# First adaLN piece summed on two engines, and w_in loaded in halves: one hybrid decoder layer on one core

## The chip, the core and the metric

One core of a Trainium2 chip runs the whole layer in one launch. TensorE (PE) multiplies, VectorE (DVE) and ScalarE (ACT) do elementwise work, SyncE (SP) issues most DMAs. The metric is the time of one execution in microseconds (us): before, the median of 3 runs is 1309.07 (1307.7 to 1309.66).

## The reference

Sequence 256, model width 2048, float32. `c` has one row, so `mod` is one vector for all positions.

```python
mod = jnp.einsum('bd,de->be', jax.nn.silu(c), w_ada[layer]) + b_ada[layer]
shift, scale, gate = jnp.split(mod, 3, axis=-1)
h = rms_norm(x, g_pre[layer]) * (1.0 + scale[:, None, :]) + shift[:, None, :]
proj = jnp.einsum('bsd,de->bse', h, w_in[layer])
q_mla, kv_a, z_mla, qkv_dil, z_dil, gl_mla, gl_dil = jnp.split(proj, IN_SPLITS, axis=-1)
a = mla_branch(q_mla, kv_a, positions, g_kv[layer], w_kv_b[layer]) * jax.nn.silu(z_mla)
y_mla = jnp.einsum('bse,ed->bsd', a, w_mla_proj[layer])
bb = dilated_branch(qkv_dil, positions) * jax.nn.silu(z_dil)
y_dil = jnp.einsum('bse,ed->bsd', bb, w_dil_proj[layer])
merged = jax.nn.sigmoid(gl_mla) * y_mla + jax.nn.sigmoid(gl_dil) * y_dil
out = jnp.einsum('bsd,de->bse', merged, w_o[layer])
x = x + gate[:, None, :] * rms_norm(out, g_post[layer])
```

w_in has 20032 columns. `mla_branch` is latent attention with 16 heads, `dilated_branch` attention of 8 heads in three groups that are merged by their softmax sums.

## The kernel before, in words

**Chunks.** The 2048 input channels lie in 16 chunks of 128 partitions. `xT[q]` is x transposed, four chunks each. For chunk k, `make_h` (L188 to 200) forms h = xT * colmul * rstdT on DVE, its high part `hTh` with the shift added on ACT (L198), and the low part `hTl` on DVE (L199). Every product of w_in runs three times: high weights by hTh, high by hTl, low by hTh (`multiply`, L237 to 245). A weight tile is loaded by SP (L215), cast to its high part `whi` on ACT (L223) and subtracted to its low part `wlo` on DVE (L224). A load holds up to four chunks of 512 columns (1 MB, `RAW`), in four buffers, and is split in two halves, with four buffers each for whi and wlo.

**Shift and scale.** h needs the columns `colsh` and `colmul` of its chunk, that is, w_ada's columns of this chunk summed over all 16 input chunks with the weights silu(c), `ccol`. `ada_steps(pi)` does this for a piece of several chunks: 16 loads of two blocks (shift, scale), each multiplied by its `ccol` and added on DVE (L164, L166) into `ada`; `finish` then sums over the partitions on PE, one product of one column with `ones` per block (L175), and DVE forms colsh and colmul. `PIECES` gives the chunks of each piece: (2, 2, 2, 2, 4, 4).

**The head.** 16 groups of columns (nine `d`, zd0, two of kva with 256 and 320 columns, zd1, three more `d`; the others 512 wide) are multiplied by the chunks known so far. In stage pi, the `VISITS[pi]` groups that have the fewest chunks are visited; a visit multiplies the chunks that the group lacks, into an accumulator in PSUM (`acc_tile`, two, of two banks each), and the result is copied by ACT at the first visit (L527) and added by DVE at later ones (L529). Between the visits the next piece's steps are issued. The last stage visits all 16 groups; behind zd0 it issues the rotary embedding `rope` (L387 to 390) of six `d` and the first dilated attention, whose products are mixed with the visits that are left.

**Start.** x is loaded in four tiles (L109), transposed by PE (L269) and copied by ACT (L270); DVE sums the squares (L273) and forms rstd by small operations (L128 to 137); `rdiag` (L282) times ones on PE (L285) spreads it to rows, copied to `rstdT`; a transposed table of rows gives biases and gains (`pt_cols`, L290).

**What sets the order.** The engines' instruction lists are static: a scheduler of the framework places the instructions on each engine, as shown below. Engines wait for each other by semaphores, a load also for the release of its buffer by the buffer's last reader.

Of the kernel before, what the change touches and what calls it, by code (L numbers as in the profile page):

```python
# [33 lines left out]
UL = 4  # L34
UK = 2
RAW = UL * 512
HALF = UK * 512
RAW_BUFS = 4
# [5 lines left out]
PIECES = (2, 2, 2, 2, 4, 4)  # L44
VISITS = (11, 9, 7, 16, 16)
# [29 lines left out]
def hybrid_block(ctx: ExitStack, tc: tile.TileContext, x, c, positions, w_ada, b_ada, g_pre, g_post,  # L75
# [8 lines left out]
    ps = ctx.enter_context(tc.tile_pool(name="ps", bufs=1, space=bass.MemoryType.PSUM))  # L84
# [16 lines left out]
    nc.scalar.dma_start(crow, c[0].rearrange("(r p) -> r p", p=P))  # L101
    nc.scalar.dma_start(tid, table[:, 0:T_ZER])
# [42 lines left out]
    def ada_steps(pi):  # L145
# [3 lines left out]
        kb = RAW // (2 * n)  # L149
# [21 lines left out]
        def finish():  # L171
            pt = tp_tile([P, 2, nk], f"pt_ada{pi}")
            for j in range(2):
                for b in range(nk):
                    T.matmul(pt[:, j, b:b + 1], acc[:, j, b * P:(b + 1) * P], ones[:, 0:1],  # L175
                             start=True, stop=True)
            V.tensor_add(colsh[:, a:a + nk], pt[:, 0, :], bsh[:, a:a + nk])
            sc = sp.tile([P, 4], F32, tag="adasc", name=f"adasc{pi}")
            V.tensor_add(sc[:, :nk], pt[:, 1, :], bsc[:, a:a + nk])
# [33 lines left out]
    def load(w, k0, nk, c0, n, name):  # L213
# [48 lines left out]
    for q in range(4):  # L262
# [36 lines left out]
    def gate_sum(n, k0):  # L299

        if k0 == 0 and n % 2 == 0:
# [6 lines left out]
            v, w_ada[0, k0 * P:(k0 + UL) * P, col:col + 512].rearrange("(k p) n -> p k n", p=P))  # L308
        for k in range(UL):
# [20 lines left out]
    gate_todo = [(n, k0) for n in range(4) for k0 in range(0, KC, UL)]  # L330
# [185 lines left out]
    def visit(gi, upto):  # L516
# [19 lines left out]
    for pi in range(len(PIECES)):  # L536
# [4 lines left out]
        if not last:  # L541
            todo = sorted(todo, key=lambda g: (have[g], g))[:VISITS[pi]]
# [65 lines left out]
    for f in range(4):  # L608
# [118 lines left out]
    step = RAW // n  # L727
    tiles = []
    for k0 in range(0, KC, step):
        tiles += load_split(w_o[0], k0, step, c0, n, f"last_{k0}")  # L730
# [36 lines left out]
```

## Time and profile before

| | |
|---|---|
| median of 3 runs | 1309.07 us (1307.7 to 1309.66) |
| profiled execution | 1308.65 us, span 1306.9 us |
| PE busy | 1263.7 us, 97% of the span |
| DVE, ACT busy | 836.7 us (64%), 590.1 us (45%) |
| DMA | 274.97 MB, mean 210 GB/s |

The span reaches from the first to the last recorded instruction. The time given for one PE instruction overlaps the next one, so a pace is read from start to start, or from a piece of the chain of waits; and a busy PE may run at half its clock, which the granted clock tells. Idle time is put down to what ended it.

### The profile page before, as it was taken

To read this page: it belongs to the slowest core of one execution; us is meant where nothing else is said; L and a number is where in the kernel's file an instruction comes from. 1 tells how busy PE (TensorE), PEld (TensorE's weight loads), DVE (VectorE), ACT (ScalarE), POOL (GpSimd) and SP (SyncE) were. 2 spreads that over 40 slices of the span, in tenths; PEclk is the share of its full clock that TensorE was granted. 3 is DMA by queue.
4 is the path that set the end of the run, shared out by engine and by line. 5 is a ranking of instruction groups with operands and counts; after the bars stand their busy time and mean duration, and the time that the engine had idled before them with its cause. 6 is when DMAs were issued, how large, how long until landed. Compare 5 with 4: busy or idle time off the path is not lost.

```text
span 1306.9 us, 16173 instructions
## 1 busy us (share of the span) xinstructions
PE 1263.7 (97%) x6239; PEld 1070.0 (82%) x6239; DVE 836.7 (64%) x1196; ACT 590.1 (45%) x746; POOL 0.2 (0%) x4
## 2 busy tenths in 40 slices
PE   3899999999999999999999999999999999999996
PEld 3688887888888888888889898898888888888886
DVE  7779999988765445539656576655444444565545
ACT  2553433433464444455545555455444444433442
POOL 0000000000000000000000000000000000000000
PEclk7999999999999999999999999999999999999999
DMA  8899988985532555425756486564555555665751
GB/s 282 275 320 300 311 305 283 317 314 170 188 130 97 193 193 194 161 73 192 238 190 238 145 264 232 172 225 160 193 193 194 193 193 193 209 211 192 258 161 65
DMA packets 155224, 274.97 MB, mean 210 GB/s; under 512 B 5830, under 2 KB 46988, under 8 KB 155148
## 3 DMA queue, kind: packets, MB, share of 16 engines
q1 hardware_dynamic: 152732, 268.62, 61.1%
q10 hardware_dynamic: 2416, 5.33, 1.2%
q8 instruction: 49, 0.80, 0.3%
q14 instruction: 27, 0.22, 0.0%
HBM read 271.83 MB, written 2.10 MB: 210 GB/s over the span
## 4 chain that ended last, share of the span: by engine, by line
PE 85%; DVE 6%; DMA 4%; ACT 2%; issue 2%; SPq 0%; DVEq 0%; ACTq 0%
PE acc_d L244 24%; PE acc_mq L244 9%; PE acc_gd L244 7%; PE acc_ym L244 7%; PE acc_gm L244 7%; PE acc_zm L244 7%; PE acc_o L244 6%; PE acc_yd L244 3%; PE acc_kv L244 3%; PE acc_zd L244 3%; DMA raw_d<-in_w_in 2%; DVE ada L166 2%; PE s_D L472 1%; PE pv_D L481 1%; PE acc_kva L244 1%
## 5 line engine op out<-in xcount | busy, mean ns | idle before, releaser
L223 ACT CAST whi_d<-raw_d 128x1024 fp32r<-128x1024 f32 x144 | 149.6, 1052 | 202.3 <-PE acc_d L244 107.0
L224 DVE TENSOR_TENSOR wlo_d<-raw_d,whi_d 128x1024 fp32r<-128x1024 f32 x144 | 174.7, 1222 | 75.1 <-ACT whi_d L223 73.9
L244 PE MATMUL acc_d<-whi_d,hTh 128*128 128x512 f32 x576 | 156.6, 394 | 7.9 <-ACT hTh L198 3.1
L244 PE MATMUL acc_d<-whi_d,hTl 128*128 128x512 f32 x576 | 157.3, 393 | 0.0
L244 PE MATMUL acc_d<-wlo_d,hTh 128*128 128x512 f32 x576 | 155.4, 392 | 0.9 <-DVE wlo_d L224 0.9
L244 PEld LDWEIGHTS acc_d<-whi_d,hTh 128*128 128x128 f32 x576 | 107.9, 189 | 32.0 <-ACT hTh L198 4.1
L244 PEld LDWEIGHTS acc_d<-wlo_d,hTh 128*128 128x128 f32 x576 | 108.5, 189 | 24.0 <-DVE wlo_d L224 1.4
L244 PEld LDWEIGHTS acc_d<-whi_d,hTl 128*128 128x128 f32 x576 | 108.4, 189 | 22.4
L166 DVE SCALAR_TENSOR_TENSOR ada<-raw_a,ccol,ada 128x512 f32<-128x512 f32 (+1 forms) x90 | 83.4, 926 | 5.8 <-DMA raw_a<-in_w_ada 4.5
L224 DVE TENSOR_TENSOR wlo_mq<-raw_mq,whi_mq 128x768 fp32r<-128x768 f32 x64 | 60.9, 956 | 36.7 <-ACT whi_mq L223 22.0
L223 ACT CAST whi_mq<-raw_mq 128x768 fp32r<-128x768 f32 x64 | 53.0, 835 | 55.9 <-PE acc_mq L244 20.0
L224 DVE TENSOR_TENSOR wlo_gm<-raw_gm,whi_gm 128x1024 fp32r<-128x1024 f32 x32 | 39.2, 1225 | 45.4 <-ACT whi_gm L223 45.4
L224 DVE TENSOR_TENSOR wlo_ym<-raw_ym,whi_ym 128x1024 fp32r<-128x1024 f32 x32 | 39.2, 1224 | 34.1 <-ACT whi_ym L223 34.1
L224 DVE TENSOR_TENSOR wlo_gd<-raw_gd,whi_gd 128x1024 fp32r<-128x1024 f32 x32 | 39.2, 1225 | 33.0 <-ACT whi_gd L223 31.3
L244 PE MATMUL acc_mq<-whi_mq,hTl 128*128 128x384 f32 x256 | 59.4, 342 | 0.0
L529 DVE TENSOR_TENSOR d<-d,acc_d 128x1024 f32<-128x1024 f32 x45 | 54.7, 1216 | 7.1 <-PE acc_d L244 7.0
L244 PE MATMUL acc_mq<-wlo_mq,hTh 128*128 128x384 f32 x256 | 57.4, 339 | 0.0
L244 PE MATMUL acc_mq<-whi_mq,hTh 128*128 128x384 f32 x256 | 56.6, 339 | 0.6 <-ACT whi_mq L223 0.6
L224 DVE TENSOR_TENSOR wlo_o<-raw_o,whi_o 128x1024 fp32r<-128x1024 f32 x28 | 34.3, 1225 | 35.3 <-ACT whi_o L223 35.3
L223 ACT CAST whi_ym<-raw_ym 128x1024 fp32r<-128x1024 f32 x32 | 33.8, 1055 | 51.1 <-PE acc_ym L244 44.3
L223 ACT CAST whi_gm<-raw_gm 128x1024 fp32r<-128x1024 f32 x32 | 33.8, 1055 | 49.6 <-PE acc_gm L244 43.9
L223 ACT CAST whi_gd<-raw_gd 128x1024 fp32r<-128x1024 f32 x32 | 33.7, 1053 | 40.7 <-PE acc_gd L244 20.3
(264 smaller groups left out, 2338.9 us busy)
## 6 DMA issues: line engine op xcount, KB each, us to landing
raw_d<-in_w_in SPq DMA_DIRECT2D x63, 1024.0 KB, 4.9
raw_mq<-in_w_in SPq DMA_DIRECT2D x32, 768.0 KB, 4.4
raw_a<-in_w_ada SPq DMA_DIRECT2D x64, 256.0 KB, 5.2
raw_a<-in_w_ada SPq DMA_DIRECT2D x32, 512.0 KB, 6.3
raw_zm<-in_w_in SPq DMA_DIRECT2D x16, 1024.0 KB, 5.0
raw_g<-in_w_ada SPq DMA_DIRECT2D x16, 1024.0 KB, 5.2
raw_gd<-in_w_in SPq DMA_DIRECT2D x16, 1024.0 KB, 4.9
raw_gm<-in_w_in SPq DMA_DIRECT2D x16, 1024.0 KB, 4.8
```

The costliest lines, as they stand in the source:

```text
L166: V.scalar_tensor_tensor(flat, w, ccol[:, kk:kk + 1], flat, op0=ALU.mult, op1=ALU.add)
L223: A.copy(whi[:, :m], raw)
L224: V.tensor_tensor(wlo[:, :m], raw, whi[:, :m].bitcast(F32), ALU.subtract)
L244: T.matmul(acc[:, t, :n], opd.get(part, k0 + k, t), wt[:, k * n:(k + 1) * n], start=start and ph == 0 and k == 0, stop=stop and ph == 2 an ...
L472: T.matmul(sc[:, i * nk:(i + 1) * nk], qk[g][:, 0, t * P:(t + 1) * P], qk[g][:, 1, 0:nk], start=True, stop=True)
L481: T.matmul(pv, pT[:, b, :], dil[2, g, quad][:, kt, hs], start=b == 0, stop=b == nb - 1)
L529: V.tensor_add(d, d, acc[:, :, lo:hi])
```

## The change

- Pieces (3, 2, 3, 2, 2, 2, 2), with visits (8, 8, 7, 7, 7, 9) ahead of the last stage: seven stages in place of six. In the last stage seven groups lack four chunks and nine lack two; before, all sixteen lacked four.
- The first piece has three chunks, and its loads are 128 x 2 x 384, one to a buffer. Even input chunks are accumulated on DVE as before. For odd ones PE multiplies the raw block (stationary) by `ccol` (one column) straight into columns of `pt_ada`, six products each. With the six for DVE's sum there are nine sets of columns, which one reduction on DVE adds.
- Loads hold two chunks of 512 columns at most (512 KB), in eight buffers, in place of four chunks (1 MB) in four. Each load is one split. The loads of `gate_sum` are halved likewise.
- The squares of the first half of x's rows go from DVE to ACT. The two first small loads go from ACT's queue to the head of SP's, three others from SP's to ACT's.
- PSUM holds three accumulators and two small tiles up to the last stage, two and four from then on.

```diff
-UL = 4
 UK = 2
-RAW = UL * 512
-HALF = UK * 512
-RAW_BUFS = 4
+RAW = UK * 512
+RAW_BUFS = 8
 W_BUFS = 4
 H_BUFS = 3
 QK_BUFS = 4
 U_BUFS = 28
 SCRATCH = 1024
-PIECES = (2, 2, 2, 2, 4, 4)
-VISITS = (11, 9, 7, 16, 16)
+PIECES = (3, 2, 3, 2, 2, 2, 2)
+VISITS = (8, 8, 7, 7, 7, 9)
...
+    head_ps = tc.tile_pool(name="psh", bufs=1, space=bass.MemoryType.PSUM)
+    banks.update(pool=head_ps.__enter__(), acc=3, b=2)
...
-    nc.scalar.dma_start(crow, c[0].rearrange("(r p) -> r p", p=P))
-    nc.scalar.dma_start(tid, table[:, 0:T_ZER])
+    nc.sync.dma_start(crow, c[0].rearrange("(r p) -> r p", p=P))
+    nc.sync.dma_start(tid, table[:, 0:T_ZER])
...
+    nc.scalar.dma_start(rows[0:32], b_ada[0, 0:4096].rearrange("(r p) -> r p", p=P))
+    nc.scalar.dma_start(rows[32:48], g_pre[0].rearrange("(r p) -> r p", p=P))
+    nc.scalar.dma_start(rows[48:52], g_kv[0].rearrange("(r p) -> r p", p=P))
...
-        kb = RAW // (2 * n)
+        kb = max(1, RAW // (2 * n))
         acc = slot([P, 2, n], f"ada{pi}")
         steps = []
         src = w_ada[0].rearrange("(k p) (j d) -> p k j d", p=P, d=D)
         flat = acc.rearrange("p j n -> p (j n)")
+        first = pi == 0
+        cnt = KC // 2 + 1 if first else 1
+        pt = tp_tile([P, cnt, 2 * nk], f"pt_ada{pi}")
+
+        def cols_of(i, block, vec):
+            for j in range(2):
+                for b in range(nk):
+                    T.matmul(pt[:, i, j * nk + b:j * nk + b + 1], block(j, b), vec, start=True, stop=True)
...
+                if first and kk % 2:
+                    cols_of(kk // 2, lambda j, b: v[:, k, j, b * P:(b + 1) * P], ccol[:, kk:kk + 1])
+                elif kk == 0:
...
+            cols_of(cnt - 1, lambda j, b: acc[:, j, b * P:(b + 1) * P], ones[:, 0:1])
+            if first:
+                tot = cp.tile([P, 2 * nk], F32, tag="adatot", name="adatot")
+                V.reduce_sum(tot, pt.rearrange("p c m -> p m c"), axis=mybir.AxisListType.X)
+            else:
+                tot = pt[:, 0, :]
+            V.tensor_add(colsh[:, a:a + nk], tot[:, 0:nk], bsh[:, a:a + nk])
             sc = sp.tile([P, 4], F32, tag="adasc", name=f"adasc{pi}")
-            V.tensor_add(sc[:, :nk], pt[:, 1, :], bsc[:, a:a + nk])
+            V.tensor_add(sc[:, :nk], tot[:, nk:2 * nk], bsc[:, a:a + nk])
...
+    def load_split(w, k0, nk, c0, n, name):
+
+        m = nk * n
         raw = wp.tile([P, RAW], F32, tag="raw", bufs=RAW_BUFS, name=f"raw_{name}")
-        nc.sync.dma_start(raw[:, :nk * n].rearrange("p (k n) -> p k n", n=n),
+        nc.sync.dma_start(raw[:, :m].rearrange("p (k n) -> p k n", n=n),
                           w[k0 * P:(k0 + nk) * P, c0:c0 + n].rearrange("(k p) n -> p k n", p=P))
-        return raw
-
-    def split_w(raw, m, name):
-
-        whi = wp.tile([P, HALF], F32R, tag="whi", bufs=W_BUFS, name=f"whi_{name}")
-        wlo = wp.tile([P, HALF], F32R, tag="wlo", bufs=W_BUFS, name=f"wlo_{name}")
-        A.copy(whi[:, :m], raw)
-        V.tensor_tensor(wlo[:, :m], raw, whi[:, :m].bitcast(F32), ALU.subtract)
+        whi = wp.tile([P, RAW], F32R, tag="whi", bufs=W_BUFS, name=f"whi_{name}")
+        wlo = wp.tile([P, RAW], F32R, tag="wlo", bufs=W_BUFS, name=f"wlo_{name}")
+        A.copy(whi[:, :m], raw[:, :m])
+        V.tensor_tensor(wlo[:, :m], raw[:, :m], whi[:, :m].bitcast(F32), ALU.subtract)
         return whi, wlo
...
+    def chunks(a, b, n):
+        step = UK if n > 256 else 2 * UK
+        return [(k, min(step, b - k)) for k in range(a, b, step)]
+
+    def run(acc, opd, w, a, b, c0, n, name):
+
+        for k, kn in chunks(a, b, n):
+            whi, wlo = load_split(w, k, kn, c0, n, f"{name}_{k}")
+            multiply(acc, opd, whi, wlo, k, kn, n, k == a, k + kn == b)
...
+            if t == 0:
+                A.activation(j[:, 0:512], xn[q][:, t, :], AF.Square, accum_out=ssx[:, t, q:q + 1])
...
+        run(acc, hT, win, a, upto, c0, n, nm)
...
+        if last:
+            head_ps.__exit__(None, None, None)
+            banks.update(pool=ctx.enter_context(tc.tile_pool(name="ps", bufs=1, space=bass.MemoryType.PSUM)),
+                         acc=2, b=4)
```

TensorE's order at the start, before; `pt_r` is the rstd product, `pt_cols` the transposed rows, `pt_ada` the column sums, `acc_d` the first visit of w_in:

```order
L285 MATMUL pt_r<-rdiag,ones 128x256
L290 MATMUL pt_cols<-tid,rows 128x52
L175 MATMUL pt_ada_252<-ones,ada_215 128x1 x4
L244 MATMUL acc_d_0_272<-whi_d_0_0_275,hTh_261 128x512 x4
L244 MATMUL acc_d_0_272<-whi_d_0_0_275,hTl_262 128x512 x4
L244 MATMUL acc_d_0_272<-wlo_d_0_0_276,hTh_261 128x512 x4
```

And now, from the same place on; `raw_a_1` is the load of input chunk 1 of the first piece:

```order
L293 MATMUL pt_r<-rdiag,ones 128x256
L298 MATMUL pt_cols<-tid,rows 128x52
L162 MATMUL pt_ada_216<-ccol,raw_a_1_220 128x1 x6
L162 MATMUL pt_ada_216<-ccol,raw_a_3_231 128x1 x6
L162 MATMUL pt_ada_216<-ccol,raw_a_5_242 128x1 x6
L162 MATMUL pt_ada_216<-ccol,raw_a_7_253 128x1 x6
L162 MATMUL pt_ada_216<-ccol,raw_a_9_264 128x1 x6
L162 MATMUL pt_ada_216<-ccol,raw_a_11_275 128x1 x6
L162 MATMUL pt_ada_216<-ccol,raw_a_13_286 128x1 x6
L162 MATMUL pt_ada_216<-ccol,raw_a_15_297 128x1 x6
L162 MATMUL pt_ada_216<-ones,ada_215 128x1 x6
L244 MATMUL acc_d_0_333<-whi_d_0_336,hTh_317 128x512 x4
```

Between the transposed rows and the column sums now stand eight groups of six one-column products, each behind its load, and the first visit has half as many products again.

ScalarE's order at the start, before; `xT` is x transposed, `whi` the cast of a load:

```order
L270 COPY xT_148<-pt_x_149 128x512
L270 COPY xT_148<-pt_x_155 128x512
L223 CAST whi_d_0_0_275<-raw_d_0_273 128x1024
L198 ACTIVATE hTh_261<-h_263,colsh 128x256
L198 ACTIVATE hTh_261<-h_267,colsh 128x256
L223 CAST whi_d_0_0_304<-raw_d_0_302 128x1024
```

And now, with the last square of x (`junk_x`) ahead of the last two copies:

```order
L275 COPY xT_131<-pt_x_138 128x512
L279 ACTIVATE junk_x_161,ssx<-xn_82 128x512
L275 COPY xT_148<-pt_x_149 128x512
L275 COPY xT_148<-pt_x_155 128x512
L210 ACTIVATE hTh_317<-h_319,colsh 128x256
L210 ACTIVATE hTh_317<-h_323,colsh 128x256
L210 ACTIVATE hTh_317<-h_327,colsh 128x256
L233 CAST whi_d_0_336<-raw_d_0_334 128x1024
```

The first cast of w_in has moved behind the `hTh`, of which there are three.

VectorE's order ahead of the first attention, before, from the embedding of `d_200` on; `rt_d` are steps of the embedding, `d_203` with `acc_d` the addition of a visit:

```order
L387 TENSOR_TENSOR rt_d_2762<-d_200,cosD 128x256
L388 TENSOR_TENSOR rt_d_2763<-d_200,sinD 128x8x16
L529 TENSOR_TENSOR d_203<-d_203,acc_d_12_2539 128x1024
L224 TENSOR_TENSOR wlo_d_12_2_2619<-raw_d_12_2612,whi_d_12_2_2618 128x1024
L389 TENSOR_TENSOR rt_d_2763<-d_200,sinD 128x8x16
L390 TENSOR_TENSOR d_200<-rt_d_2762,rt_d_2763 128x8x32
L224 TENSOR_TENSOR wlo_d_12_0_2651<-raw_d_12_2648,whi_d_12_0_2650 128x1024
L387 TENSOR_TENSOR rt_d_2768<-d_201,cosD 128x256
L388 TENSOR_TENSOR rt_d_2769<-d_201,sinD 128x8x16
L389 TENSOR_TENSOR rt_d_2769<-d_201,sinD 128x8x16
```

And now, from the same embedding on:

```order
L395 TENSOR_TENSOR rt_d_3112<-d_200,cosD 128x256
L396 TENSOR_TENSOR rt_d_3113<-d_200,sinD 128x8x16
L535 TENSOR_TENSOR d_203<-d_203,acc_d_12_2967 128x1024
L234 TENSOR_TENSOR wlo_d_14_3069<-raw_d_14_3066,whi_d_14_3068 128x1024
L397 TENSOR_TENSOR rt_d_3113<-d_200,sinD 128x8x16
L398 TENSOR_TENSOR d_200<-rt_d_3112,rt_d_3113 128x8x32
L535 TENSOR_TENSOR d_204<-d_204,acc_d_14_3005 128x1024
L234 TENSOR_TENSOR wlo_zd_14_3089<-raw_zd_14_3086,whi_zd_14_3088 128x1024
L395 TENSOR_TENSOR rt_d_3118<-d_201,cosD 128x256
L535 TENSOR_TENSOR d_205<-d_205,acc_d_14_3025 128x1024
```

Between two additions stands one split in place of two; the steps of the embedding are the same.

## Rows read from the trace of the kernel before

**Rows 1.** The page's first table: busy us, share of the span, instructions.

```profile
PE 1263.7 (97%) x6239; PEld 1070.0 (82%) x6239; DVE 836.7 (64%) x1196; ACT 590.1 (45%) x746; POOL 0.2 (0%) x4
```

**Rows 2.** PE in order of time, 0 to 32 us: start, us, line, operation.

```profile
7.25 5.73 PE L269 MATMUL pt_x<-tid,xn 128*128 128x128 f32 x32
15.92 0.67 PE L285 MATMUL pt_r<-rdiag,ones 128*128 128x256 f32 x2 [2.94 <-DVE rdiag L282]
...
26.36 1.84 PE L175 MATMUL pt_ada<-ones,ada 128*128 128x1 f32 x8 [9.57 <-DVE ada L166]
29.86 2.08 PE L244 MATMUL acc_d<-whi_d,hTh 128*128 128x512 f32 x4 [1.66 <-ACT hTh L198]
```

**Rows 3.** Stretches: busy us of each engine, granted clock, DMA share, GB/s.

```profile
20.00:25.00 5.00, 0.00 (x0) 0.00 (x0) 4.79 (x7) 1.04 (x1) 0.00 (x0) 0.50 1.08 360
29.86:35.30 5.44, 5.44 (x13) 4.28 (x14) 3.92 (x6) 1.28 (x2) 0.00 (x0) 0.50 0.59 169
35.30:59.02 23.72, 19.89 (x85) 15.47 (x84) 17.25 (x20) 13.99 (x14) 0.00 (x0) 1.00 0.87 287
59.02:286.53 227.51, 221.47 (x1050) 185.53 (x1048) 206.84 (x224) 95.92 (x106) 0.00 (x0) 1.00 0.89 305
345.00:420.00 75.00, 74.86 (x433) 62.94 (x432) 42.95 (x81) 42.16 (x65) 0.00 (x0) 1.00 0.37 127
```

**Rows 4.** PE's waits, 0 to 420 us: total, times, longest.

```profile
PE pt_ada L175 <- DVE ada L166: 10.7, 2, 9.6
...
PE acc_d L244 <- ACT hTh L198: 3.1, 2, 1.7
...
PE acc_d L244 <- ACT whi_d L223: 2.6, 1, 2.6
PE acc_d L244 <- DVE d L529: 1.9, 3, 0.8
PE acc_zd L244 <- ACT whi_zd L223: 1.6, 1, 1.6
PE acc_d L244 <- DVE wlo_d L224: 0.9, 1, 0.9
```

**Rows 5.** The chain of waits: start, us, instructions.

```profile
214.69 49.26 PE acc_d L244 x216
...
269.39 6.39 PE acc_kva L244 x48
...
286.69 1.68 PE pt_ada L175 x16
```

**Rows 6.** ACT in order of time, 0 to 36 us.

```profile
11.70 2.05 ACT L270 COPY xT<-pt_x 128x512 f32<-128x512 f32 x4 [0.16 <-PE pt_x L269]
23.36 1.04 ACT L223 CAST whi_d<-raw_d 128x1024 fp32r<-128x1024 f32 x1 [9.61 <-DMA raw_d<-in_w_in]
29.30 0.91 ACT L198 ACTIVATE hTh<-h,colsh 128x256 fp32r<-128x256 f32 x2 [4.89 <-DVE h L197]
```

**Rows 7.** ACT's squares of this shape, elsewhere: busy us, mean ns.

```profile
L576 ACT ACTIVATE junk_kv<-kva 128x512 f32<-128x512 f32 x2 | 1.3, 628 | 0.0
```

**Rows 8.** DVE in order of time: the sum of squares and rdiag.

```profile
11.40 0.16 DVE L276 TENSOR_REDUCE ssq<-ssx 128x2 f32<-128x8 f32 x1
...
15.30 0.47 DVE L282 TENSOR_SCALAR rdiag<-tid,rstd 128x128 f32<-128x128 f32 x2
```

**Rows 9.** The accumulations: duration ns minimum, median, maximum, and forms.

```profile
L166 DVE SCALAR_TENSOR_TENSOR ada<-raw_a,ccol,ada x90: 737/752/1286, 13.4 to 279.1; 128x512 f32<-128x512 f32 x60, 128x1024 f32<-128x1024 f32 x30
```

**Rows 10.** Stretches with the transposes alone.

```profile
7.20:11.30 4.10, 4.05 (x19) 4.05 (x20) 1.00 1.07 366
11.50:12.80 1.30, 1.30 (x14) 1.24 (x12) 1.00 1.05 340
```

**Rows 11.** DVE, 286 to 345 us: the additions of visits.

```profile
L529 DVE TENSOR_TENSOR d<-d,acc_d 128x1024 f32<-128x1024 f32 x11 | 13.4, 1218 | 5.2 <-PE acc_d L244 5.2
```

More of the change, by code (lines that the diff above doesn't have):

```diff
@@ L83, in hybrid_block @@
     sp = ctx.enter_context(tc.tile_pool(name="sp", bufs=2))
-    ps = ctx.enter_context(tc.tile_pool(name="ps", bufs=1, space=bass.MemoryType.PSUM))
+    banks = {}
     def slot(shape, name, dt=F32):
@@ L89, in acc_tile @@
     def acc_tile(name):
-        return ps.tile([P, 2, 512], F32, tag="acc", bufs=2, name=name)
+        return banks["pool"].tile([P, 2, 512], F32, tag="acc", bufs=banks["acc"], name=name)
     def tp_tile(shape, name):
-        return ps.tile(shape, F32, tag="b", bufs=4, name=name)
+        return banks["pool"].tile(shape, F32, tag="b", bufs=banks["b"], name=name)
+    head_ps = tc.tile_pool(name="psh", bufs=1, space=bass.MemoryType.PSUM)
+    banks.update(pool=head_ps.__enter__(), acc=3, b=2)
     xr = x[0].rearrange("(t p) d -> p t d", p=P)
@@ L171, in finish @@
         def finish():
[L172 to L177, printed above, removed]
+            cols_of(cnt - 1, lambda j, b: acc[:, j, b * P:(b + 1) * P], ones[:, 0:1])
[5 more added lines that the diff above has]
+            V.tensor_add(colsh[:, a:a + nk], tot[:, 0:nk], bsh[:, a:a + nk])
             sc = sp.tile([P, 4], F32, tag="adasc", name=f"adasc{pi}")
-            V.tensor_add(sc[:, :nk], pt[:, 1, :], bsc[:, a:a + nk])
+            V.tensor_add(sc[:, :nk], tot[:, nk:2 * nk], bsc[:, a:a + nk])
             V.scalar_tensor_tensor(colmul[:, a:a + nk], sc[:, :nk], 1.0, gpre[:, a:a + nk],
@@ L245, in multiply @@
                              start=start and ph == 0 and k == 0, stop=stop and ph == 2 and k == nk - 1)
-    def unit(acc, opd, w, k0, nk, c0, n, start, stop, name):
-        for k, kn, whi, wlo in load_split(w, k0, nk, c0, n, name):
-            multiply(acc, opd, whi, wlo, k, kn, n, start and k == k0, stop and k + kn == k0 + nk)
+    def chunks(a, b, n):
[5 more added lines that the diff above has]
+            multiply(acc, opd, whi, wlo, k, kn, n, k == a, k + kn == b)
     def group(opd, w, nk, c0, n, name):
         acc = acc_tile(f"acc_{name}")
-        for k0 in range(0, nk, UL):
-            unit(acc, opd, w, k0, UL, c0, n, k0 == 0, k0 + UL == nk, f"{name}_{k0}")
+        run(acc, opd, w, 0, nk, c0, n, name)
         return acc
@@ L307, in gate_sum @@
         nc.sync.dma_start(
-            v, w_ada[0, k0 * P:(k0 + UL) * P, col:col + 512].rearrange("(k p) n -> p k n", p=P))
-        for k in range(UL):
+            v, w_ada[0, k0 * P:(k0 + UK) * P, col:col + 512].rearrange("(k p) n -> p k n", p=P))
+        for k in range(UK):
             kk = k0 + k
@@ L328, in gate_finish @@
                 V.tensor_mul(gg[m], gg[m], b)
-    gate_todo = [(n, k0) for n in range(4) for k0 in range(0, KC, UL)]
+    gate_todo = [(n, k0) for n in range(4) for k0 in range(0, KC, UK)]
     def gate_some(cnt):
@@ L540, in hybrid_block @@
         todo = list(range(len(head)))
-        if not last:
+        if last:
+            head_ps.__exit__(None, None, None)
+            banks.update(pool=ctx.enter_context(tc.tile_pool(name="ps", bufs=1, space=bass.MemoryType.PSUM)),
+                         acc=2, b=4)
+        else:
             todo = sorted(todo, key=lambda g: (have[g], g))[:VISITS[pi]]
@@ L614, in hybrid_block @@
             j = 2 * f + pr
-            gate_some(KC // UL // 2)
+            gate_some(KC // UK // 2)
             acc = group(hT, win, KC, j * 384, 384, f"mq{j}")
@@ L719, in hybrid_block @@
         acc = acc_tile(f"acc_o{i}")
-        step = RAW // n
-        for k0 in range(0, KC, step):
-            unit(acc, mT, w_o[0], k0, step, c0, n, k0 == 0, k0 + step == KC, f"o{i}_{k0}")
+        run(acc, mT, w_o[0], 0, KC, c0, n, f"o{i}")
         for t in range(2):
@@ L726, in hybrid_block @@
     acc = acc_tile("acc_last")
[L727 to L730, printed above, removed]
+    tiles = [(k, kn) + load_split(w_o[0], k, kn, c0, n, f"last_{k}") for k, kn in chunks(0, KC, n)]
     for t in range(2):
```

21 lines of the change are left out of this document (3 added, 18 removed).

## The prediction

> **What bounds the kernel now.** I began with the page's first table: TensorE (PE) is busy 97% of the span [rows 1]. Where PE is full, a change can only move the time in which it is not yet running or runs at half clock, so the next view was PE's own order of time over the start [rows 2]: 32 transposes, a hole from 12.98 to 15.92 us, the rstd product, a hole of 9.57 us that ends when DVE has finished its accumulation `ada`, the first column sums at 26.36, the first w_in product at 29.86. Third, the table by stretches [rows 3]: from 29.86 to 35.30 the granted clock is 0.50 (1.2 GHz), afterwards 1.00 (2.4 GHz), and DMA delivers 287 and 305 GB/s. Fourth, PE's waits up to 420 us [rows 4]. Behind the head PE has next to nothing left to give (74.86 of 75 us from 345 on [rows 3]), so the forecast lies in the first 290 us and in the entry to the first attention.
>
> To put one number on the start, I count PE against its steady pace, read from the chain: 216 matmuls in 49.26 us, 0.228 (0.227 in longer pieces), kva 48 in 6.39, 0.133, warm column sums 16 in 1.68, 0.105 [rows 5]. From 29.86 to 59.02 stand 8 visits of 12 matmuls: 96 x 0.227 = 21.8 of 29.2 us, 7.4 lost. From 59.02 to 286.53 stand 1008 matmuls (864 wide ones, 196.1 us; 144 of kva, 19.2) and 40 column sums (4.2): 219.5 of 227.5, 8.0 lost. So the kernel before works as if PE had begun at 29.86 + 15.4 = 45.3 us and never waited. The same sum for the changed kernel is the forecast; products, column sums and everything behind 290 us are the same in number.
>
> What are the 15.4 made of? Half clock: 5.44 us held 13 matmuls, 2.95 us at full pace, 2.5 lost [rows 3]. The waits behind the first product [rows 4]: for hTh 3.1 less 1.7 at the very first, 1.4; pt_ada 10.7 less 9.6, 1.1; wlo 0.9; casts of loads that came late 2.6 and 1.6; an accumulator that DVE had not yet emptied 1.9. That is 9.5, with the clock 12.0; 3.4 have no name.
>
> **The change part by part.**
>
> First product, by data. Before, the first cast waited for its load until 23.36 [rows 6]. By then 2.1 MB of x, 4.2 MB of first piece and 0.5 MB of w_in had landed. Three chunks instead of two make the first piece 6.3 MB, so its last load has 8.4 MB ahead of or in it, 1.6 more: at 360 GB/s, the rate of 20 to 25 us [rows 3], 4.5 us, 27.9. Of the 16 loads the last eight wait for a buffer (four of them for PE, the rest for DVE): 1 to 3 us, I take 2, so 30.0.
>
> First product, by engines. Half of the squares go to ACT, each 0.63 us for this shape [rows 7] and as much again between them for the copies, which alone ended at 13.75 [rows 6]; the last square ends near 14, and the sum of squares moves from 11.40 [rows 8] to there. The chain to rdiag took from 11.40 to 15.77 [rows 8] with three accumulations inside, up to 0.75 each; without them some 2.4, with the one of 768 elements that now lies in it 3.5 (between 0.75 for 512 and 1.29 for 1024 [rows 9] I take 1.02). So the rstd product moves from 15.92 to about 17.5, and PE, which takes its odd chunks behind it and the transposed rows, starts on them at 18.9. They are 48 products of one column, two instructions each: 96. At 0.105 they take 10.1 us, to 29.0, and then follow the loads to 30.0; at 0.213 (8 in 1.84 at 26.36 [rows 2], and the period of the first transposes [rows 10]) 20.4, to 39.3. DVE has 8 x 1.02 = 8.2 us in place of 16 x 0.75 and is no longer last.
>
> Behind the last load: 12 instructions of the last odd chunk and 12 of the DVE sum, 24 x 0.105 = 2.5. From the end of the column sums (28.20) to the first product were 1.66 us. Added now: the reduction 0.16, a third hTh 0.41, and the first cast, which stands behind the hTh in ACT's order and no longer ahead of them, 1.04 [rows 6]: 3.3. First product at 30.0 + 2.5 + 3.3 = 35.8 if data sets it. PE has then been busy for long, so the 2.5 us of half clock are gone; it is the term on which the forecast leans.
>
> The stages. The balance is products against bytes: in stage one 24 units of a chunk and 512 columns, 6 x 0.227 = 1.36 us each, are 32.6 us, for 24 x 0.262 MB of w_in and 4.2 MB of the next piece, 10.5 MB: 322 GB/s. Stage two, reckoned alike, has 48.5 us for 15.6 MB (the next piece has three chunks), also 322; the others 278 to 286. Before, every stage stood between 300 and 322, against 287 and 305 delivered [rows 3]. With eight buffers full when PE starts (about 3 MB), stages one and two need 23.1 MB in 81 us, 285 GB/s: casts wait for no load. A third accumulator takes the 1.9 us for DVE's additions. Left are the turns of the pieces, six in place of five: (1.4 + 1.1) x 6/5 = 3.0, and 0.9 for wlo: 3.9. Of the 3.4 without a name I keep half, 1.7. Bounds: 1.5 (nothing but wlo and a few turns) to 9.5 + 3.4 (all as before).
>
> Entry of the first attention. The last stage now multiplies two chunks for nine columns, 2.72 us a visit in place of 5.44, while each still costs DVE an addition of 1.22 [rows 11], and six ropes lie between. I count some 20 us of DVE against 16 of PE, and a lead of about 5 from the visits ahead: nothing to 2 us, I take 0.5 together with the swap of PSUM pools. Bounds 0 and 5.
>
> Hidden edits: thirteen additions fewer (75 visits, now 62) and single loads of 512 KB behind the head, where DVE is busy 42.95 of 75 us and DMA 0.37 [rows 3]: 0, and 1 either way. Without that cover a late load costs a few tenths each.
>
> Sum: 35.8 + 3.9 + 1.7 + 0.5 = 41.9 against 45.3, -3.4 us. The profiled execution took 1308.65 us (span 1306.9), within 0.5 of the median 1309.07: 1305.2.
>
> **What the clock does, and a rule against the change.** In the trace the transposes run 19 in 4.05 us at first, 0.213, and 14 in 1.30 afterwards, 0.093 [rows 10]: transposes alone brought the pace up. After the holes behind 12.98 the granted clock is 0.50 from 20 us [rows 3], so PE's odd chunks will start at 1.2 GHz. Whether one-column products raise it no row shows; nearest are the transposes, with the same 128x128 load of the array for each instruction, and I go by them. The Trainium skill, "TensorE: Matmul & The Clock Gate", Part 4: PE-mode transpose, says that in transposes the full clock does not engage. Those of this trace contradict it; if it holds for the one-column products all the same, the time is rival B's.
>
> **Rivals.** A is the forecast: the loads, or nearly they, set the first product, 1305.2; if half of the odd chunks run cold (48 x 0.213 + 48 x 0.105 = 15.3, to 34.2, first product near 38.8), -0.4. Its range is -8 to 0.5 us, 1300.6 to 1309.2.
>
> B, the other side: the clock stays at 1.2 GHz through the one-column stream. Then PE is the bound of the first piece: 18.9 + 20.4 + 12 x 0.213 + 3.3 = 45.2, and the half clock is still paid, 2.5, as the first wide products have to raise it; loads are all there, so the 1.7 are not. 45.2 + 2.5 + 3.9 + 0.5 = 52.1, +6.8: 1315.5 (+4 to +10). It decides from the point at which more than about 60 of 96 instructions run at 0.213. For it: 0.213 at 26.36 [rows 2]. Against: the transposes.
>
> C: loads of half the size and a three-chunk stage starve PE again. Stages one and two move 26.1 MB; without the stock of 3 MB, at 305 GB/s, 85.6 us against 81.1, +4.5: about +1, 1309.7, no change that can be told. For it: SP issues each load only when a buffer is released by DVE. Against: the first piece's loads of 256 KB ran at 360 GB/s [rows 3], more than the stages' mixture. The Trainium skill, "DMA: Bandwidth & Descriptors", Measured (HBM to SBUF), wants DMAs batched to 1 MiB; by it the smaller loads would lose rate, and the time is C's. The loads of 256 KB in this trace do not show it.
>
> **How the numbers follow.** A 0.54, B 0.33, C 0.13. 0.2%, 2.6 us, is about what a measurement of this kernel can tell from no change. A is beyond that in 0.68 of its cases, within it in 0.25; C mostly within; B nearly always slower. Faster 0.37 + 0.03 + 0.01 = 0.41; within 0.14 + 0.08 + 0.02 = 0.24; slower 0.03 + 0.02 + 0.30 = 0.35 (A, C, B in this order). The range goes from A's low end to a little above B's value, 1300.5 to 1316.8; A's own is 1300.6 to 1309.2.
>
> **What would show it.** In PE's order of time: odd chunks from about 19 us, their period (0.105 or 0.213) and the granted clock in 20 to 40 us; first wide product near 36 (A) or 45 (B), and its first visits at 0.227 or double. In the waits: casts behind loads near zero, hTh and pt_ada some 3 us. In the table by stretches: 305 GB/s or more in the first 80 us. At the attention: how long PE stands before its first transposes. A is wrong if the first product comes after 40 us, or if it comes at 36 and the time has not fallen: then the stages lose more than 6 us.

## The result and the profile after

The changed kernel takes 1316.9 us (median of 4 runs, 1315.42 to 1317.71), beside 1309.37 (4 runs) before: a ratio of 1.0056, interval 1.0039 to 1.0073. It is slower, by about 7 us, where 3.4 us faster was forecast. The figure is close to that of rival B, 1315.5.

PE in order of time, the changed kernel; these rows answer to [rows 2]:

```profile
16.67 1.19 PE L293 MATMUL pt_r<-rdiag,ones 128*128 128x256 f32 x2 [3.73 <-DVE rdiag L290]
...
18.38 20.64 PE L162 MATMUL pt_ada<-ccol,raw_a 128*128 128x1 f32 x96 [0.24 <-DVE rstdT L294]
38.88 2.70 PE L162 MATMUL pt_ada<-ones,ada 128*128 128x1 f32 x12
45.15 2.07 PE L244 MATMUL acc_d<-whi_d,hTh 128*128 128x512 f32 x4 [3.56 <-ACT whi_d L233]
...
52.73 1.07 PE L244 MATMUL acc_d<-whi_d,hTl 128*128 128x512 f32 x4
```

The odd input chunks start at 18.38 us, near the forecast (18.9). Their 96 instructions then reach to 38.88, 0.213 us each from start to start, and the first w_in product stands at 45.15, not at 35.8. The stretches, answering to [rows 3] (busy us of each engine, granted clock, DMA share, GB/s):

```profile
18.40:38.00 19.60, 19.60 (x92) 19.60 (x93) 5.12 (x6) 0.00 (x0) 0.00 (x0) 0.50 0.82 256
45.15:51.80 6.65, 6.65 (x19) 5.25 (x19) 6.19 (x8) 1.93 (x3) 0.00 (x0) 0.61 0.60 169
60.00:280.00 220.00, 220.00 (x1042) 185.52 (x1041) 185.22 (x235) 103.88 (x123) 0.00 (x0) 1.00 0.91 298
```

Through the whole stream PE is busy 19.60 of 19.60 us at a granted clock of 0.50. It rises only within the first visits of w_in: 18 products take 6.65 us, 4.09 at full pace, 2.56 lost as before. From 60 to 280 us PE is busy throughout, which the kernel before was not. PE's waits up to 450 us, answering to [rows 4]:

```profile
PE pt_r L293 <- DVE rdiag L290: 3.7, 1, 3.7
PE acc_d L244 <- ACT whi_d L233: 3.6, 1, 3.6
...
PE acc_d L244 <- DVE d L535: 1.4, 1, 1.4
```

No wait for a late load of w_in is left. So the change lost at the start, gained in the stages, and there is a third place. To add them up I sum, over PE's instructions, what each one's distance to the next start exceeds the median of its form in the trace of before (us, from the first w_in product on, so the half clock is in the second column; `zm` is the first MLA group, `gd` the first gate group behind MLA):

| | first w_in product | lost up to 280 | 280 to 345 | 345 to zm | zm to gd | end of the last product |
|---|---|---|---|---|---|---|
| before | 29.86 | 15.06 | 0.18 | 3.57 | 12.81 | 1297.32 |
| after | 45.15 | 2.59 | 1.92 | 4.11 | 14.96 | 1304.08 |
| difference | +15.29 | -12.47 | +1.74 | +0.54 | +2.15 | +6.76 |

How finely forms are told apart moves the columns from 345 on, in both kernels alike; the differences stay. The columns add up to 7.25; four column sums fewer behind the first product are 0.42, the rest is within 0.1.

The third place is MLA, which the forecast put at nothing. VectorE there, the changed kernel (`gacc` are the gate sums, L656 the mask and maximum of a softmax, L658 its scaling):

```profile
654.99 2.32 DVE L322 SCALAR_TENSOR_TENSOR gacc<-raw_g,ccol,gacc 128x512 f32<-128x512 f32 x3
657.23 0.42 DVE L656 CUSTOM_DVE_ANT_0 sm_M<-s_M,msk 128x256 f32<-128x256 f32 x1
...
657.78 0.75 DVE L322 SCALAR_TENSOR_TENSOR gacc<-raw_g,ccol,gacc 128x512 f32<-128x512 f32 x1
658.45 0.16 DVE L658 TENSOR_SCALAR st_M<-st_M 128x2 f32<-128x2 f32 x1
```

And PE:

```profile
657.43 0.85 PE L244 MATMUL acc_zm<-whi_zm,hTl 128*128 128x512 f32 x3
659.30 0.44 PE L446 MATMUL pt_pM<-tid,sm_M 128*128 128x128 f32 x2 [1.01 <-ACT sm_M L662]
```

Three gate accumulations stand ahead of the mask and one more ahead of the scaling; PE stands 1.01 us for the exponential that follows. It happens in two places (about 658 and 820 us), 2.5 us in all.

### The profile page after: what moved, and what is told of

Same layout as the page of the kernel before. It is cut to its first block, busy times and chain, and to the rows that moved or that the text cites. A ratio compares the mean times of both kernels' runs of the same rounds, so it can differ in the third digit from the quotient of the medians.

```text
span 1313.5 us, 16974 instructions
## 1 busy us (share of the span) xinstructions
PE 1283.7 (98%) x6335; PEld 1090.3 (83%) x6335; DVE 815.9 (62%) x1203; ACT 596.9 (45%) x770; POOL 0.2 (0%) x4
## 5 line engine op out<-in xcount | busy, mean ns | idle before, releaser
L233 ACT CAST whi_d<-raw_d 128x1024 fp32r<-128x1024 f32 (+1 forms) x156 | 152.8, 987 | 179.6 <-PE acc_d L244 152.8
L234 DVE TENSOR_TENSOR wlo_d<-raw_d,whi_d 128x1024 fp32r<-128x1024 f32 (+1 forms) x156 | 176.3, 1139 | 70.4 <-ACT whi_d L233 68.4
L177 DVE SCALAR_TENSOR_TENSOR ada<-raw_a,ccol,ada 128x512 f32<-128x512 f32 (+1 forms) x97 | 78.4, 808 | 20.3 <-DMA raw_a<-in_w_ada 19.4
L234 DVE TENSOR_TENSOR wlo_o<-raw_o,whi_o 128x1024 fp32r<-128x1024 f32 x28 | 34.2, 1224 | 35.4 <-ACT whi_o L233 35.4
L234 DVE TENSOR_TENSOR wlo_zm<-raw_zm,whi_zm 128x1024 fp32r<-128x1024 f32 x32 | 39.2, 1224 | 18.8 <-ACT whi_zm L233 17.1
```

The lines of the kernel that those rows point to most:

```text
L233: A.copy(whi[:, :m], raw[:, :m])
L234: V.tensor_tensor(wlo[:, :m], raw[:, :m], whi[:, :m].bitcast(F32), ALU.subtract)
```

## The experiments

Ratios are to the kernel before on the same chip, with the 95% interval. Theory: one-column products run at the clock that PE has, do not raise it and do not hold it.

**E1: the first piece on DVE alone.**

```diff
-        first = pi == 0
+        first = False
```

> The changed kernel with the first piece summed on DVE alone (PE only sums DVE's one sum over the partitions). Theory 1: PE's one-column stream at 1.2 GHz was the bound of the first piece (first w_in product at 45.2 us). Then the first product moves to about 17.5 + 13 x 1.02 + 12 x 0.213 + 3.3 = 36.6 us, and the time falls by 8 to 9 us against the changed kernel, to about 1308.5, no longer slower than before. Rival: the stages (smaller loads, more turns) are what costs, then the time stays within 3 us of the changed kernel's 1316.9 although the first product comes earlier.

Measured: 1305.71 us, ratio 0.9968 (0.9958 to 0.9979), faster than before. PE at the start:

```profile
31.06 2.72 PE L162 MATMUL pt_ada<-ones,ada 128*128 128x1 f32 x12 [10.23 <-DVE ada L177]
35.36 2.07 PE L244 MATMUL acc_d<-whi_d,hTh 128*128 128x512 f32 x4 [1.58 <-ACT hTh L210]
```

The first product comes 9.8 us earlier than in the changed kernel, the last one ends 9.1 us earlier. PE's share of the first piece costs that much, and the rest of the change, taken together, is a gain. The stages are not to blame.

**E2: extra wide products ahead of the stream.**

```diff
+    dum = acc_tile("dum")
+    for i in range(9):
+        T.matmul(dum[:, i % 2, :], ident, xn[i % 4][:, 0, :], start=True, stop=True)
```

> The changed kernel with nine extra products of 128 x 512 (x times the identity, never read), most of them in PE's hole between the transposes and the rstd product. Theory 1, one-column products neither raise the clock nor hold it: the stream starts at 0.105 us an instruction and falls back to 0.213 within it; first w_in product between 40 and 44 us. Rival 2, the clock was only lost in the hole and one-column products would hold it: 0.105 throughout, first product at 35 to 37 us and the time 8 us below the changed kernel's.

Measured (one run): 1316.31 us. The one-column products alone, in three stretches of the stream, which starts at 21.89:

```profile
22.00:26.50 4.50, 4.50 (x40) 4.50 (x40) 0.96 0.54 158
26.50:27.50 1.00, 1.00 (x7) 1.00 (x6) 0.50 0.74 218
28.00:38.00 10.00, 10.00 (x49) 10.00 (x48) 0.50 0.88 289
```

At the full clock one takes 0.11 us (40 in 4.50). At 26.1 the granted clock falls, with PE busy without a gap before and behind, and they take 0.21 (49 in 10.00). First product at 44.80. Rival 2 is out: the clock is not merely lost in the hole ahead, the stream does not hold it.

**E3: one extra wide product to each odd chunk.**

```diff
                     cols_of(kk // 2, lambda j, b: v[:, k, j, b * P:(b + 1) * P], ccol[:, kk:kk + 1])
+                    T.matmul(dum[:, 0, :], v[:, k, 0, 0:P], xn[0][:, 0, :], start=True, stop=True)
```

> The changed kernel with one extra product of 128 x 512 (raw block times x, never read) to each odd input chunk of the first piece; five of them stand between groups of one-column products. Theory 1: wide products bring the clock up, so the stream runs at 0.105 from there on, although there is more work: first w_in product at 37 to 41 us, 4 to 8 us below the changed kernel. Rival 3, the 0.213 comes from the operands (raw blocks fresh from DMA, one column) and not from the clock: the stream keeps 0.213, the extra work adds 3 to 7 us, first product near 49, time near 1321.

Measured: 1318.73 us, ratio 1.007 (1.0044 to 1.0096). Three of the extra products stand ahead of the stream, five between its groups. The stretches:

```profile
18.60:23.90 5.30, 5.30 (x49) 5.30 (x48) 2.81 (x3) 0.00 (x0) 0.00 (x0) 0.99 0.91 294
24.00:45.00 21.00, 21.00 (x70) 15.84 (x70) 2.03 (x2) 1.04 (x1) 0.00 (x0) 0.50 0.72 216
```

The first 48 instructions run at 0.11 us (5.30 us at 0.99), from fresh raw blocks, so rival 3 is out. But my theory's other half failed too: behind 24 us groups of twelve one-column instructions and two of 512 columns alternate, PE is busy all the time, and the clock stays at 0.50; first product at 47.24. A wide product here and there does not bring it back.

**E4: the raw block as the moving operand.** The sum over the odd chunks then stands in PSUM as one row.

```diff
-                    cols_of(kk // 2, lambda j, b: v[:, k, j, b * P:(b + 1) * P], ccol[:, kk:kk + 1])
+                    for j in range(2):
+                        T.matmul(row[0:1, j, 0:n], ccol[:, kk:kk + 1], v[:, k, j, :],
+                                 start=kk == 1, stop=kk == KC - 1)
```

> The changed kernel with PE's half of the first piece turned round: ccol is the stationary operand (one column) and the raw block moves, 2 x 384 columns an input chunk, summed in PSUM over the eight odd chunks into one row, which twelve one-column products and six more for DVE's sum bring to columns. Theory 1: these wide products bring the clock up; an odd chunk costs 1.3 us at 2.4 GHz (2.6 at 1.2), so PE keeps up with the loads; first w_in product at 37 to 41 us, time 1308 to 1312. If the clock stays at 0.50 all the same, an odd chunk takes 2.6 us, the eight 21 us, and the first product comes at 44 to 47 us, no better than the changed kernel.

Measured: 1306.53 us, ratio 0.9972 (0.9959 to 0.9985). PE in order of time, and then the stretches of the rows, of the column sums, of their tail with the hole behind it, and of the first w_in products:

```profile
25.69 1.45 PE L175 MATMUL ada_row<-raw_a,ccol 128*1 128x384 f32 x4 [0.66 <-DMA raw_a<-in_w_ada]
...
28.17 1.45 PE L175 MATMUL ada_row<-raw_a,ccol 128*1 128x384 f32 x4
...
36.55 2.07 PE L253 MATMUL acc_d<-whi_d,hTh 128*128 128x512 f32 x4 [1.58 <-ACT hTh L219]
```

```profile
17.64:29.60 11.96, 9.49 (x29) 2.05 (x28) 5.55 (x7) 0.00 (x0) 0.00 (x0) 1.00 1.07 373
30.50:32.30 1.80, 1.80 (x12) 1.72 (x12) 0.00 (x0) 1.41 (x2) 0.00 (x0) 1.00 1.09 367
33.00:36.50 3.50, 1.97 (x8) 1.84 (x8) 1.42 (x6) 0.51 (x2) 0.00 (x0) 0.50 0.98 335
36.55:42.00 5.45, 5.45 (x13) 4.29 (x14) 5.45 (x10) 2.20 (x4) 0.00 (x0) 0.50 0.36 109
```

Here PE waits for loads (0.66 us ahead of this chunk), is busy 9.49 of 11.96 us only, and keeps 1.00. The rows started when the clock was at 1.00 already, so that they raise it is not shown. It falls in the tail of one-column products and short holes, and is 0.50 for the first w_in products. A chunk takes 1.4 us, below the 2.1 in which two chunks land, so the loads set the pace, as the forecast had meant. That the first product (36.55) is no earlier than E1's (35.36) lies in the tail: 6.8 us from 28.17, where the last row products start, to the end of the column sums. So the row form takes back what the one-column form cost; beside leaving the piece to DVE (E1's 0.9968) no gain is shown.

**E5: E1 with the old pieces.**

```diff
-PIECES = (3, 2, 3, 2, 2, 2, 2)
-VISITS = (8, 8, 7, 7, 7, 9)
+PIECES = (2, 2, 2, 2, 4, 4)
+VISITS = (11, 9, 7, 16, 16)
```

> The version with the first piece on DVE alone, and the old pieces (2, 2, 2, 2, 4, 4) with their visits: what is left of the change are the eight buffers of 512 KB, three accumulators, the squares on ACT. Theory buffers: the stages lost little in the changed kernel because loads run ahead in eight buffers; then the first product comes at about 31 us, the stages lose 3 to 5 us more than none, and the time falls 2 to 4 us below that version's 1305.7. Rival pieces: the three-chunk first piece lets the loads get ahead while PE is not yet running, and a first stage of two chunks starves again as in the kernel before (12.9 us lost behind its first product); then the time is 1305 to 1309.

Measured: 1302.66 us, ratio 0.9933 (0.992 to 0.9946). PE at the start:

```profile
27.02 1.86 PE L162 MATMUL pt_ada<-ones,ada 128*128 128x1 f32 x8 [5.74 <-DVE ada L177]
30.46 2.08 PE L244 MATMUL acc_d<-whi_d,hTh 128*128 128x512 f32 x4 [1.57 <-ACT hTh L210]
```

With the start of before (30.46), 4.61 us are lost up to 280, where before lost 15.06: theory buffers, not pieces. Against E1 the start gains 4.9 and gives back 1.6 in the stages and 2.6 between 280 and 345; MLA takes 1.7 less. The interval lies below E1's whole: beside the old pieces the new pieces with their visits are themselves a loss, of 2.4 us at the last product.

**E6: E1 with two accumulators.**

```diff
-    banks.update(pool=head_ps.__enter__(), acc=3, b=2)
+    banks.update(pool=head_ps.__enter__(), acc=2, b=4)
```

> The version with the first piece on DVE alone, with two accumulators and four small tiles in PSUM from the start. Theory: the third accumulator takes the waits for DVE's additions, 1.9 us in the kernel before; without it the time rises by 1 to 3 us to about 1307.5. Rival: the loads alone set the stages' losses, and the time stays within 0.7 us of 1305.7.

Measured: 1307.13 us, ratio 0.9963 (0.9948 to 0.9978), which overlaps E1's 0.9968; 3.85 us lost up to 280, beside 3.03. Of these 2.66 lie in the first visits at half clock (E1: 3.01); behind them E6 loses 1.19, nearly all at one wait put down to a cast, and E1 0.03. So the third accumulator is worth 1.2 us at most in these traces, and the times show no gain by it; and no wait for DVE's addition stands in E6's stages, so it is not what took the 1.9 us of before away.

**E7: E1 with the gate sums spread.** The kernel that ran is not quite what its expectation says: it issues two loads at each of two places of a pair of heads, not one at each of four.

```diff
-            gate_some(KC // UK // 2)
+            gate_some(2)
             acc = group(hT, win, KC, j * 384, 384, f"mq{j}")
...
+            gate_some(2)
             acc = group(ckv, wkv, 4, j * 512, 512, f"kv{j}")
```

> The version with the first piece on DVE alone, with the gate sums' loads issued one at a time at four places of each pair of heads in place of four at once, so that at most three and not five of their accumulations stand in the eight VectorE rows ahead of a softmax. Theory: in the changed kernel PE waited twice, 1.5 and 1.0 us, for a softmax that stood behind five accumulations of 0.67 us on DVE, and once 0.4 for a rope; these waits go, and the time falls by 1.5 to 3 us to about 1303.5. Rival: the softmax waits for something else (ACT's cast ahead of the exponential), and the time stays within 1 us of 1305.7.

Measured: 1302.19 us, ratio 0.9932 (0.9919 to 0.9944). VectorE at the same softmax:

```profile
643.79 0.74 DVE L322 SCALAR_TENSOR_TENSOR gacc<-raw_g,ccol,gacc 128x512 f32<-128x512 f32 x1
645.10 0.42 DVE L657 CUSTOM_DVE_ANT_0 sm_M<-s_M,msk 128x256 f32<-128x256 f32 x1 [0.56 <-PE s_M L651]
...
645.78 0.17 DVE L659 TENSOR_SCALAR st_M<-st_M 128x2 f32<-128x2 f32 x1
```

One accumulation is left ahead of the mask, which now waits for PE, and none ahead of the scaling. From zm to gd PE takes 344.13 us, in E1 347.30. Of the 4.6 us between the ends of the last products 3.2 are this; 1.5 lie in the first visits, where the clock rose earlier (1.53 lost up to 280 in place of 3.03), which the edit does not touch.

**E8: the kernel before, with PE's share alone.** The lines of `cols_of` and of the reduction from the change, in the old kernel (32 products).

```diff
-                if kk == 0:
+                if first and kk % 2:
+                    cols_of(kk // 2, lambda j, b: v[:, k, j, b * P:(b + 1) * P], ccol[:, kk:kk + 1])
+                elif kk == 0:
```

> The kernel before with one part of the change alone: PE takes the odd input chunks of its first piece (two chunks) by one-column products, DVE the even ones. Theory: 32 products of two instructions at 0.213 us are 13.6 us from about 17 us on, so the column sums come at 31 and not at 26.4, the first w_in product near 34.5 in place of 29.9, the time 3 to 5 us above before, about 1313. Rival: with two chunks the stream is short enough that DVE's relief wins; first product at 28 or earlier, time 1307 to 1309.

Measured: 1315.33 us, ratio 1.0031 (1.0019 to 1.0042): slower. PE at the start, and two of its waits up to 560 us:

```profile
15.49 11.71 PE L161 MATMUL pt_ada<-ccol,raw_a 128*128 128x1 f32 x64
27.06 1.84 PE L161 MATMUL pt_ada<-ones,ada 128*128 128x1 f32 x8
32.54 2.08 PE L255 MATMUL acc_d<-whi_d,hTh 128*128 128x512 f32 x4 [3.63 <-ACT whi_d L234]
```

```profile
PE acc_d L255 <- ACT whi_d L234: 6.5, 3, 3.6
PE acc_zd L255 <- ACT whi_zd L234: 2.3, 1, 2.3
```

The stream is shorter than I expected, 64 in 11.57 us (0.18, so part of it at the full clock); the column sums come at 27.06, later than 26.36, and the first product at 32.54. Of the waits for casts 3.6 are those of the first product, whose cast has moved to the end as in the changed kernel; behind it are 5.2, before 4.2 [rows 4]. Up to 280 us 18.25 are lost, 3.2 more than before. In two stretches of the stages, each behind a wait of PE, the clock is at half, which happens nowhere in the stages of before:

```profile
75.84:79.26 3.42, 3.42 (x10) 2.66 (x9) 3.27 (x4) 2.51 (x3) 0.00 (x0) 0.50 1.08 365
219.20:222.62 3.42, 3.42 (x9) 2.65 (x9) 3.42 (x7) 1.97 (x4) 0.00 (x0) 0.50 0.62 235
```

They cost 3.0 us; the first visits lose 2.1 more than before, the waits elsewhere 1.9 less. That this part alone is no gain is shown; why PE's waits changed is not.

**E9: E4 with a shorter tail, gates as in E7.** DVE's sum goes into the same row, six one-column products follow.

```diff
+                for j in range(2):
+                    T.matmul(row[0:1, j, 0:n], ones[:, 0:1], acc[:, j, :], start=False, stop=True)
+                A.copy(rs[:, 0, :], row[0:1, 0, 0:n])
+                V.tensor_copy(rs[:, 1, :], row[0:1, 1, 0:n])
```

> PE's half of the first piece with the raw blocks moving (as in the version with rows), and DVE's sum brought into the same row by two more products of 384 columns, so that only six one-column products follow; the gate sums spread as in the version before. Theory: PE keeps 2.4 GHz through the first piece, the tail of 6.8 us behind the last row product shrinks by 2 us, first w_in product near 34.5 us; half clock is still paid behind it, since PE stands for some 3 us ahead of it. Time against the version with rows: 2 us from the start and about 3 from the gates, so 0.9935 of the kernel before. Rival: DVE or the loads set the first product, 36 us or later, and the time is 0.995 or more.

Measured: 1300.11 us, ratio 0.9921 (0.9899 to 0.9944).

```profile
27.75 1.45 PE L175 MATMUL ada_row<-raw_a,ccol 128*1 128x384 f32 x4 [0.65 <-DMA raw_a<-in_w_ada]
29.03 1.45 PE L189 MATMUL ada_row<-ada,ones 128*1 128x384 f32 x4
...
34.30 1.77 PE L251 MATMUL acc_d<-whi_d,hTh 128*128 128x512 f32 x4 [1.58 <-ACT hTh L217]
```

The first product stands at 34.30, as expected, and 1.74 us are lost up to 280. The interval overlaps that of E7 (0.9919 to 0.9944), which leaves the piece to DVE: that PE's rows gain over it is not shown.

**E10: E9 with two extra products in the holes ahead of w_in.**

```diff
+                T.matmul(dum[:, 0, :], acc[:, 0, 0:P], xn[0][:, 0, :], start=True, stop=True)
...
+                T.matmul(dum[0:nk, 1, :], colsh[:, 0:nk], xn[0][:, 0, :], start=True, stop=True)
```

> The same with two extra products of 512 columns (never read), one behind DVE's sum and one that waits for colsh, in PE's holes ahead of the first w_in product. Theory: the clock is still at 1.00 when the first w_in product starts, so its 2.5 us of half clock go; about 2 us below the same kernel without them, 0.992 of the kernel before. Rival: the clock falls in the short holes all the same, or falls for the one-column products; then the time is the same or up to 1 us higher.

Measured: 1299.7 us, ratio 0.9916 (0.9891 to 0.9941): the same as E9 within the interval. PE ahead of the first visit, and the stretches:

```profile
33.52 1.02 PE L204 MATMUL dum<-xn,colsh 128*3 128x512 f32 x2 [0.25 <-DVE colsh L198]
34.85 1.19 PE L255 MATMUL acc_d<-whi_d,hTh 128*128 128x512 f32 x4 [0.31 <-ACT hTh L221]
35.88 1.08 PE L255 MATMUL acc_d<-whi_d,hTl 128*128 128x512 f32 x4
```

```profile
30.00:35.00 5.00, 4.44 (x21) 2.03 (x20) 3.99 (x10) 2.01 (x5) 0.00 (x0) 1.00 1.07 365
35.00:40.00 5.00, 5.00 (x23) 4.10 (x24) 4.60 (x9) 2.79 (x5) 0.00 (x0) 1.00 0.95 305
```

The clock stays at 1.00, the first visit runs at full pace (1.19 us from the issue of its first four products to their end, before 2.08 [rows 2]), 0.83 us are lost up to 280. But the extra work puts the first product at 34.85, and in E9 the half clock had cost only 1.7 us: 0.3 us are left at the end of the last product. The mechanism held; the 2 us did not come.

**E11: E7 with four buffers of 512 KB.**

```diff
-RAW_BUFS = 8
+RAW_BUFS = 4
```

> The version with the first piece on DVE and the gate sums spread, with four load buffers of 512 KB in place of eight. Theory buffers: what took the stages' losses from 12.9 us to about 2 is that eight loads run ahead; with four the casts wait for loads again, and the time rises by 4 us or more. Rival: the smaller unit alone (a buffer is free after one split) did it; the time stays within 1.5 us.

Measured: 1361.53 us, ratio 1.0385 (1.0349 to 1.042). The stretch of the stages, in E7 and then here, and PE's waits here up to 345 us:

```profile
60.00:280.00 220.00, 220.00 (x1042) 185.49 (x1041) 185.91 (x235) 100.13 (x118) 0.00 (x0) 1.00 0.91 302
60.00:280.00 220.00, 202.09 (x919) 166.90 (x919) 156.99 (x196) 88.58 (x109) 0.00 (x0) 0.97 0.78 253
```

```profile
PE acc_d L244 <- ACT whi_d L233: 10.1, 8, 3.7
PE acc_zd L244 <- ACT whi_zd L233: 8.9, 4, 5.1
...
PE acc_kva L244 <- ACT whi_kva L233: 5.0, 3, 3.5
```

With half of the load buffers DMA delivers 253 GB/s in the stages, where E7 had 302, and PE loses 35.4 us up to 280, in E7 1.53. But this kernel has half of the buffer memory of before (2 MB in place of 4), so it tells that eight are needed, not that halves beat four loads of 1 MB of the same memory; for that E5 stands beside the kernel before, and there the accumulators differ too, so it is likely and not shown alone.

## Why the prediction was wrong, point by point

- **The step that failed** is the rate of one-column products: "Whether one-column products raise it no row shows; nearest are the transposes ... and I go by them". They took 0.213 us and not 0.105 throughout, 20.5 us and not 10.1; PE and not the loads set the first product (45.15, not 35.8), and the half clock was paid as well (2.56 us, taken as gone because PE would have "been busy for long"; it was busy for 20 us, and the clock stayed). E2 and E3 show that the stream loses a full clock, E4 that the same sum with the raw block moving keeps it. The bound of 39.3 us for the end of the stream, from the other nearest row, was 38.88: both ends stood in the text, and I chose the wrong one. The products at 26.36 [rows 2] were of the same form as those in question, the transposes were not; but they took 1.84 us only, so no row of before could tell what a long stream of them does. The reading of the transposes holds, though their later pace is 0.109 us from start to start and not 0.093: the stretch counted two that only reach into it. The Trainium skill's sentence ("TensorE: Matmul & The Clock Gate", Part 4: PE-mode transpose), which I set aside for transposes, does not speak of one-column products; for them the time came out as if it did.
- **Start up to the stream**: 18.9 forecast, 18.38 measured. The last squares ended earlier than 14: the sum of squares stood at 12.89.
- **Behind the last load**: 3.3 forecast from the column sums to the first product, 3.57 measured, with the cast last as read from the order.
- **The stages** were mis-sized the other way: 3.9 + 1.7 forecast beside the half clock; measured 2.59 with its 2.56, so next to nothing. The waits at turns of pieces are gone too; that PE has work over a turn when loads run ahead and several visits' casts are ready is argued, and in E5, with the old pieces, one such wait of 1.7 us is left. The third accumulator, to which I gave 1.9, is worth 1.2 at most in the traces (E6), and not by the waits that I meant.
- **Entry of the attention**: 0.5 forecast, 1.74 measured, of it 1.41 one wait for an addition on DVE. It is there with two accumulators from the start too (E6: 1.91 lost from 280 to 345), so their number is not its cause. The swap of pools, which E6 keeps, probably is: the wait stands at the first product behind it, and ends with the addition of the visit just before, DVE's first line here, PE's second:

```profile
324.08 1.22 DVE L535 TENSOR_TENSOR d<-d,acc_d 128x1024 f32<-128x1024 f32 x1 [0.53 <-PE acc_d L244]
325.45 1.17 PE L244 MATMUL acc_d<-whi_d,hTh 128*128 128x512 f32 x4 [1.41 <-DVE d L535]
```

Before and in E8, which have one pool, 0.18 and 0.21 us are lost from 280 to 345. In E5 the same wait is 2.43, and a stretch at half clock follows, so 4.49 are lost. No run leaves the swap alone out.
- **Hidden edits at 0, 1 either way**: MLA lost 2.15 more, at two softmaxes behind the accumulations of the halved gate loads. "DVE is busy 42.95 of 75 us" was true of its share and said nothing of these places; E7, which spreads the loads, takes the cost away. In E5, with the loads as in the change, the two waits are 1.3 us together, so their size depends on where the queue meets the softmax.
- **Rivals**: B came, at 45.2 for the first product (45.15) and +6.8 (the last product ends 6.76 later). Its first product is right by its mechanism; that the whole sum is right is luck, by two errors that cancel: 3.8 us too much in the stages (6.4 for 2.59), 3.9 too little behind 280 (0.5 for 4.43). C did not come: no late load is left, and loads of 512 KB run at 298 GB/s in the stages, beside 305 before, with PE never short of them.

## What to carry to other kernels

Price an operation at both ends of the clock; look for a row of the same form before a neighbour with the same load of the array, and where neither lasts long enough to tell, say that the choice is open. Work given to a waiting engine is not free when that engine is at half clock and its form of work keeps it there: turn the product round so that the long operand moves, or leave the work where it was, which here was as fast (E4 and E1, E9 and E7). And read an off-path engine's queue at the places where the critical engine waits for it; its mean share says nothing there.

## What the runs showed of the hardware

- Granted clock and form of work: PE busy 100% with one-column products at 0.50 for 20 us (after), falling from 1.00 in the midst of them (E2, which started them at 21.89, at 26.1; E8, which started at 15.49, at 17.8); with two wide instructions to twelve of them still 0.50 over 21 us (E3); with rows of 384 columns and waits between, busy 79%, 1.00 (E4, 17.64 to 29.60).
- Load buffers: 302 GB/s with eight of 512 KB (E7, 60 to 280 us), 253 with four (E11, the same code otherwise), and 0.9932 and 1.0385 of the time before.
- What beats both kernels most: E10 and E9, 0.9916 and 0.9921 of the time before; 0.986 of the changed kernel by the quotient of the ratios (0.9916 / 1.0056). E5's old pieces and E7's spread gates were not run together.
